# Buffers of the first MLP's first norms, the place of the down projection's last right operand, and late transposes behind the next mixer's projections

## The chip, the cores and the metric

One core of one Trainium2 chip. The metric is the time of one execution on the device in microseconds (us), as the median of three runs. TensorE (PE, with its weight loads as PEld), VectorE (DVE), ScalarE (ACT), GpSimd (POOL) and the DMA queue of SyncE (SP, or SPq) each work through a fixed list of instructions in order and wait for each other by semaphores.

## The reference

Two layers on 1024 tokens of width 1024, all in fp32. Each layer normalizes the stream, mixes tokens, adds the normalized result back, and does the same with an MLP of inner width 4096:

```python
for layer in range(DEPTH):
    u = rmsnorm(h, norm_mix_pre[layer])
    if layer % 2 == 0:
        mix = hybrid_ab_mixer(u, ...)      # gated delta rule beside an RWKV7 recurrence
    else:
        mix = retention_mixer(u, ...)      # chunkwise retention with rotary positions
    h = h + rmsnorm(mix, norm_mix_post[layer])
    u = rmsnorm(h, norm_mlp_pre[layer])
    f = jnp.square(jax.nn.relu(u @ mlp_w_up[layer])) @ mlp_w_down[layer]
    h = h + rmsnorm(f, norm_mlp_post[layer])
```

## The kernel before

**Products.** An fp32 factor is split into a rounded part (hi, a cast on ACT) and the rest (lo, a subtraction on DVE), `split_in` at L1174 and L1175; a product is three matmuls, hi by hi, lo by hi, hi by lo. The MLP multiplies in quarters with seven products in place of eight. Up projection: `product`, L1302 to L1304; its results go to DRAM as `hds[n]`. Down projection: seven products n in the order 1, 5, 6, 3, 7, 2, 4 (L1472). Each has eight steps h of 24 matmuls (`three`, L1444 to L1446): the left operand comes from `hds[n][h]` (L1517), the right one from `right(n, h)` (L1422), which loads blocks of `w_down` of 512 KB (`block`, L1419) and keeps running differences in R0 to R7 and B22, made by POOL (`plus`, L1413). Results are summed in `facc` (`flush`, also L1413).

**Norms.** The 1024 tokens are eight tiles of 128, here called tokens 0 to 7. After each mixer and each MLP a token goes through `post_norm_in`: load of the stream (L1181), square with sum on ACT (L240), small one-column operations on DVE (L244 to L248), multiply by the norm's weights on POOL (L1183), scale and add on DVE (L1184), store (L1185). Then `pre_norm`: square of the new stream on ACT, L266 on DVE, eight transposes on PE (L272), and the transposed tile is split into hi and lo for the next products. In MLP 0 `normed` first loads the mixer's output (`fd`, L1267), which the mixer stored at L1149.

**Generators.** `normed` and `finish` are generators; lists of tokens (`steps`, `end`, `behind`) say when each goes on between products.

**Memory.** `region((a, b))` names kilobytes a to b of each SBUF partition; an area deals them out, and a tile in used memory waits until the last users of the old one are done. Bounds of 8 KB units give the number in a tile's name (piece104 begins at 104 KB). The order of each engine's list, SP's loads and stores included, is fixed when the kernel is built, by a scheduler that plans by a cost model of its own.

## Time and profile before

| | |
|---|---|
| runs | 3387.65, 3390.89, 3395.80 us, median 3390.89 |
| profiled execution | 3386.39 us, of it span 3384.7 us |
| PE busy | 92% of the span |
| PEld, DVE, ACT, POOL busy | 79%, 59%, 39%, 39% |
| DMA | 423.72 MB, mean 125 GB/s |
| loads of `w_down` | 96 of 512 KB |

Times inside the kernel count from the start of the span. The layers follow each other: mixer 0 to about 1121 us, its norms to 1208, MLP 0 to 1850, mixer 1, and MLP 1 to the end, its up projection until 3040. In a view of windows a row gives busy time and, in brackets, the number of instructions for each engine, then the granted clock of PE as a share of 2.4 GHz (0.50 is 1.2 GHz), the DMA engines' share and rate. In a timeline a row gives start, length, engine, line, operation and, in square brackets, the idle time before it and what ended it.

### The profile page before, as it was taken

Reading aid. Unit: us, or ns where it says so; the run is one execution under the profiler, and the core shown is the slowest. Engines: PE = TensorE matmul, PEld = TensorE weight load, DVE = VectorE, ACT = ScalarE, POOL = GpSimd, SP = SyncE. Lnnn points to the kernel's source line nnn. Section 1 sums busy time; section 2 is a strip of 40 time slices with the busy share of each in tenths; the row PEclk is TensorE's granted clock in tenths of the full one; section 3 lists DMA queues with packets and bytes.
Section 4 is the critical chain, followed back from the end, with each engine's and each line's share of the span. In section 5 each row is a group of like instructions: output and inputs, shape, how many; then the busy total and the mean of one; then the engine's idle time right before and its main releaser. Section 6 shows DMA issues by size and latency. Waiting matters only on the chain.

```text
span 3384.7 us, 44433 instructions
## 1 busy us (share of the span) xinstructions
PE 3119.0 (92%) x16424; PEld 2661.3 (79%) x16424; DVE 1990.7 (59%) x3399; ACT 1311.8 (39%) x2336; POOL 1307.9 (39%) x1577
## 2 busy tenths in 40 slices
PE   8899899899998379999997999999999989999997
PEld 6677788787877258887886889998999968878885
DVE  6445555545633466557468665567655775547467
ACT  5332333323232345543334333334333355543333
POOL 1663363365520247657043111002110147657044
PEclk9898979988897689999998999999999989999998
DMA  5221222221241456566254322235222356566353
GB/s 165 66 66 35 71 61 63 67 55 52 61 119 54 146 155 191 184 239 251 100 193 164 116 81 82 88 107 162 82 81 88 106 177 195 179 242 236 104 187 137
DMA packets 401691, 423.72 MB, mean 125 GB/s; under 512 B 69569, under 2 KB 303937, under 8 KB 400961
## 3 DMA queue, kind: packets, MB, share of 16 engines
q1 hardware_dynamic: 401472, 420.88, 39.1%
q8 instruction: 129, 2.11, 0.3%
q14 instruction: 90, 0.73, 0.1%
HBM read 322.77 MB, written 98.04 MB: 124 GB/s over the span
## 4 chain that ended last, share of the span: by engine, by line
PE 52%; DVE 5%; DMA 4%; issue 1%; ACT 1%; POOL 1%; SPq 0%; DVEq 0%; ACTq 0%; POOLq 0%
PE bank L185 20%; PE bank L1445 5%; PE bank L1303 5%; PE bank L1444 5%; PE bank L1302 5%; PE bank L1446 5%; PE bank L1304 5%; DMA piece<-in_mlp_w_down_dram 1%; DVE piece L1175 1%; DMA piece<-ud 1%; DMA piece<-in_mlp_w_up_dram 1%; DMA piece<-hd 1%; DVE piece L1501 1%; POOL piece L1413 0%; DVE piece L205 0%
## 5 line engine op out<-in xcount | busy, mean ns | idle before, releaser
L185 PE MATMUL bank<-piece,piece 128*128 128x512 f32 (+7 forms) x10032 | 1751.0, 336 | 64.9 <-ACT piece L312 15.5
L185 PEld LDWEIGHTS bank<-piece,piece 128*128 128x128 f32 (+1 forms) x10032 | 1508.9, 200 | 275.4 <-issue 34.4
L1175 DVE TENSOR_TENSOR piece<-piece,piece 128x512 fp32r<-128x512 f32 (+2 forms) x436 | 581.1, 1357 | 268.3 <-ACT piece L1174 262.1
L1174 ACT CAST piece<-piece 128x512 fp32r<-128x512 f32 (+2 forms) x436 | 354.7, 838 | 565.5 <-PE bank L1303 212.8
L1302 PE MATMUL bank<-piece,piece 128*128 128x512 f32 x896 | 353.0, 395 | 15.2 <-ACT piece L1174 9.4
L1445 PE MATMUL bank<-piece,piece 128*128 128x512 f32 x896 | 354.1, 395 | 13.3 <-DVE piece L1175 13.3
L1303 PE MATMUL bank<-piece,piece 128*128 128x512 f32 x896 | 352.5, 393 | 1.9 <-DVE piece L1234 1.9
L1304 PE MATMUL bank<-piece,piece 128*128 128x512 f32 x896 | 349.9, 394 | 1.3 <-DVE piece L1175 1.2
L1446 PE MATMUL bank<-piece,piece 128*128 128x512 f32 x896 | 351.1, 393 | 0.0
L205 DVE TENSOR_TENSOR piece<-piece,piece 128x1024 fp32r<-128x1024 f32 x202 | 258.2, 1279 | 144.3 <-ACT piece L204 139.6
L1444 PE MATMUL bank<-piece 128*128 128x512 f32 x832 | 327.6, 394 | 15.3 <-ACT piece L1174 15.3
L204 ACT CAST piece<-piece 128x1024 fp32r<-128x1024 f32 x204 | 213.5, 1048 | 295.3 <-PE bank L185 275.8
L1413 POOL TENSOR_TENSOR piece<-piece,piece 128x1024 f32<-128x1024 f32 (+1 forms) x72 | 210.8, 2946 | 262.1 <-DMA piece<-in_mlp_w_down_dram 225.5
L620 POOL TENSOR_TENSOR piece<-piece 128x120 f32<-128x120 f32 (+22 forms) x496 | 183.6, 370 | 229.6 <-DMA piece<-dm 194.1
L1577 POOL TENSOR_TENSOR piece<-piece,piece 128x512 f32<-128x512 f32 x32 | 64.4, 2013 | 530.3 <-DVE piece L1576 475.8
L1302 PEld LDWEIGHTS bank<-piece,piece 128*128 128x128 f32 x896 | 170.4, 190 | 53.1 <-ACT piece L1174 10.4
L1445 PEld LDWEIGHTS bank<-piece,piece 128*128 128x128 f32 x896 | 171.2, 191 | 50.4 <-DVE piece L1175 14.4
L1183 POOL TENSOR_TENSOR piece<-piece,piece 128x1024 f32<-128x1024 f32 x28 | 78.5, 2812 | 330.4 <-ACT piece L240 199.3
L624 POOL TENSOR_TENSOR piece<-piece,piece 128x120 f32<-128x120 f32 (+22 forms) x496 | 190.1, 383 | 37.4
L1304 PEld LDWEIGHTS bank<-piece,piece 128*128 128x128 f32 x896 | 170.3, 190 | 38.2 <-DVE piece L1175 2.7
L1303 PEld LDWEIGHTS bank<-piece,piece 128*128 128x128 f32 x896 | 170.5, 190 | 37.6 <-DVE piece L1234 2.2
L1446 PEld LDWEIGHTS bank<-piece,piece 128*128 128x128 f32 x896 | 170.6, 190 | 35.1
(242 smaller groups left out, 3197.1 us busy)
## 6 DMA issues: line engine op xcount, KB each, us to landing
hd<-piece SPq DMA_DIRECT2D x208, 256.0 KB
piece<-hd SPq DMA_DIRECT2D x104, 512.0 KB
piece<-in_mlp_w_down_dram SPq DMA_DIRECT2D x96, 512.0 KB
piece<-in_ret_w_in_dram SPq DMA_DIRECT2D x96, 512.0 KB
piece<-in_mlp_w_up_dram SPq DMA_DIRECT2D x32, 1024.0 KB
piece<-in_ab_w_in_dram SPq DMA_DIRECT2D x60, 512.0 KB
piece<-in_ret_w_out_dram SPq DMA_DIRECT2D x32, 512.0 KB
h<-piece SPq DMA_DIRECT2D x24, 512.0 KB
```

The lines of the kernel that those rows point to most:

```text
L185: PE.matmul(ps, lhsT, rhs, start=start, stop=stop)
L204: ACT.copy(hi, raw)
L205: eng.tensor_tensor(out=lo, in0=raw, in1=hi, op=ALU.subtract)
L1174: ACT.copy(hi, src)
L1175: eng.tensor_tensor(out=lo, in0=src, in1=hi, op=ALU.subtract)
L1302: PE.matmul(ps, w[0][:, k, :], u[0][:, k, :], start=start and k == 0, stop=False, skip_group_check=True)
L1303: PE.matmul(ps, w[0][:, k, :], u[1][:, k, :], start=False, stop=False, skip_group_check=True)
L1304: PE.matmul(ps, w[1][:, k, :], u[0][:, k, :], start=False, stop=stop and k == 3, skip_group_check=True)
L1413: eng.tensor_tensor(out=out, in0=a, in1=b, op=op)
L1444: PE.matmul(ps, a[0], b[0], start=first, stop=False)
L1445: PE.matmul(ps, a[1], b[0], start=False, stop=False)
L1446: PE.matmul(ps, a[0], b[1], start=False, stop=last)
```

## The change

Three parts.

First norms of MLP 0: tokens 0 to 3 get buffers of their own (104 to 112 for `nf`, 112 to 120 for `nx`), tokens 4 to 7 keep those at 172 and 180. Layer 1 stays as it was.

Last right operand: the difference R[h] minus block (1, 0, h), which product 4 uses, is made in product 2, which loads the same block as its own right operand. Product 4 loads none; the loads of `w_down` fall from 96 to 80. In layer 1 the split of this operand moves into product 2 too; its left operand there has four buffers, not six. R0 to R3 now lie at 120 to 136 and R4 to R7 at 104 to 120, and the sums of tokens 4 to 7 at 72 to 88, those of tokens 0 to 3 at 88 to 104.

Late transposes: in MLP 0's last product tokens 4 and 5 no longer go as far as their transposes; the generators of tokens 4 to 7 are handed on in a list, and layer 1 takes one entry of it behind each of its first projections. Its tiles lie at other places, and its output tiles are made when first written. In PE's list the 24 matmuls of the first projection of layer 1 (q) now come ahead of the transposes of token 4, which stood ahead of them; the transposes of token 5 follow, then k.

```diff
--- before.py
+++ after.py
@@ -1198,15 +1198,16 @@
             bs = [region((a, a + 16)).area() for a in (140, 156)]
             b11, b21 = ([mk(a, [P, 4, HT], f"b{i}", F32R) for i in "HL"] for a in bs)
             if layer:
-                wrow, nrm, tmp = region((24, 32)).area(2), region((32, 40)).area(2), region((172, 180)).area()
-                nfa = None
+                wrow, tmp = region((24, 32)).area(2), region((172, 180)).area()
+                nrms = [region((32, 40)).area(2)] * 2
                 at = dict(t1=104, t2=120, t3=40, b22=56, t4=88)
                 ring = region((180, 204)).area(6)
                 raw_at, res_at, ops_at = (0, 16), (72, 88), ((40, 56), (180, 204), (56, 64))
                 left_at, norm_at = (0, 16), ((172, 180), (64, 72))
             else:
-                wrow, nrm, tmp = region((32, 40)).area(2), region((180, 188)).area(2), region((24, 32)).area()
-                nfa = region((172, 180)).area(2)
+                wrow, tmp = region((32, 40)).area(2), region((24, 32)).area()
+                nfas = [region((a, a + 8)).area(2) for a in (104, 172)]
+                nrms = [region((a, a + 8)).area(2) for a in (112, 180)]
                 at = dict(t1=104, t2=120, t3=188, b22=72, t4=88)
                 ring = region((40, 72)).area(8)
                 raw_at, res_at, ops_at = (172, 188), (0, 16), ((188, 204), (40, 72))
@@ -1263,10 +1264,10 @@
                 if layer:
                     f = late[t - 4]
                 else:
-                    f = mk(nfa, [P, D], "nf")
+                    f = mk(nfas[t // 4], [P, D], "nf")
                     SP.dma_start(f, fd[t])
                 junk = mk(tp, [P, HT], "junk").bitcast(BF16)
-                xt = post_norm_in(nrm, f, res, mid, t, w1, junk)
+                xt = post_norm_in(nrms[t // 4], f, res, mid, t, w1, junk)
                 yield
                 yield from pre_norm(f, xt, w2, (psx if t < 4 else psn, "pd"),
                                     to_pair(ug, t) if t < 4 else combine(t))
@@ -1396,14 +1397,15 @@
 
 
             sh = [P, 2, HT]
-            left = region(left_at, (16, 24)).area(6)
+            left = region(left_at, (16, 24)).area(6) if layer == 0 else region(left_at).area(4)
             stream = region((24, 40)).area(4)
             ring = region(*ops_at).area(6)
-            R = [mk(region((104, 136)).area() if 0 else at_, sh, f"R{i}") for at_ in [region((104, 136)).area()] for i in range(8)]
+            atr = region((120, 136), (104, 120)).area()
+            R = [mk(atr, sh, f"R{i}") for i in range(8)]
             at22 = region((140, 172)).area()
             B22 = [mk(at22, sh, f"B{i}") for i in range(8)]
             fp = region((72, 104)).area()
-            fp = region((72, 104)).area()
+            fp = region((88, 104), (72, 88)).area()
             facc = [mk(fp, [P, D], f"fa{t}") for t in range(8)]
             c11, c12 = ([facc[t][:, i * HT : i * HT + HT] for t in range(4)] for i in range(2))
             c21, c22 = ([facc[t + 4][:, i * HT : i * HT + HT] for t in range(4)] for i in range(2))
@@ -1434,10 +1436,15 @@
                     b = block(0, 1, h)
                     plus(POOL, b, B22[h], b, ALU.subtract)
                     return b
+                if n == 4:
+                    return R[h]
                 b = block(1, 0, h)
-                if n == 4:
-                    plus(POOL, R[h], R[h], b, ALU.subtract)
-                    return R[h]
+                plus(POOL, R[h], R[h], b, ALU.subtract)
+                if layer:
+                    hi, lo = mk(his, sh, f"bh{h}", F32R), mk(los, sh, f"bl{h}", F32R)
+                    ACT.copy(hi, R[h])
+                    DVE.tensor_tensor(out=lo, in0=R[h], in1=hi, op=ALU.subtract)
+                    parts.append((hi, lo))
                 return b
 
             def three(ps, a, b, first, last):
@@ -1469,7 +1476,10 @@
                 for i in range(t, max(t - 3, -1), -1):
                     next(run[i], None)
 
+            parts = []
             for n in (1, 5, 6, 3, 7, 2, 4):
+                if n == 2 and layer:
+                    his, los = region((140, 172)).area(), region((16, 24), (120, 136), (104, 112)).area()
                 if n == 2:
 
                     ugn = pair(region((140, 172)).area(), "u") if layer == 0 else None
@@ -1492,14 +1502,6 @@
                 pss = [mk(psd, [P, HT], "pd") for _ in range(4)]
                 if n == 4 and layer:
                     atl, athl = region(left_at).area(2), region(*ops_at).area(2)
-                    parts = []
-                    his, los = region((140, 172)).area(), region((16, 24), (104, 128)).area()
-                    for h in range(8):
-                        b = right(4, h)
-                        hi, lo = mk(his, sh, f"bh{h}", F32R), mk(los, sh, f"bl{h}", F32R)
-                        ACT.copy(hi, b)
-                        DVE.tensor_tensor(out=lo, in0=b, in1=hi, op=ALU.subtract)
-                        parts.append((hi, lo))
                     for t in range(4):
                         raw = mk(atl, [P, 16, P], "a")
                         SP.dma_start(raw, hq[:, t])
@@ -1526,23 +1528,24 @@
                             if n == 2:
                                 end(t)
                             elif n == 4:
-                                end(t + 4)
+                                for i in range(t + 4, max(t + 2, 3), -1):
+                                    next(run[i])
                 if n == 2:
                     for t in (3, 2, 3):
                         next(run[t], None)
-            return ugn, [run[i] for i in (7, 6, 7)]
+            return ugn, [[run[7], run[4]], [run[5]], [run[6]], [run[7]]]
 
 
     def layer1(ug, behind, late, meanwhile):
         if True:
-            rest, early = region((72, 136)), region((40, 72))
+            rest, early = region((96, 136)), region((40, 72))
+            fp, Sp = region((72, 88)).area(1), region((88, 96)).area(1)
             yp, Yp, sp = region((0, 24)).area(3), region((24, 32)).area(2), region((136, 140)).area(1)
             wp[0] = region((32, 40)).area(2)
             weight_area(172, 204)
             cp, tp = early.area(1), early.area(2)
-            fp, hp = rest.area(1), rest.area(2)
-            f = [mk(fp, [P, D], f"rf{t}") for t in range(4)]
-            late.extend(f)
+            hp = rest.area(2)
+            f = []
             psj, psc, pst = bank_area(4, 5, 6), bank_area(1, 2, 3), bank_area(7, 0)
             us = tiles(ug)
             tabs = {}
@@ -1557,7 +1560,7 @@
 
             def table(c, i, n):
                 return tabs[c][:, i : i + n]
-            S = [mk(fp, [P, 256], f"S{h}") for h in range(NH_RET)]
+            S = [mk(Sp, [P, 256], f"S{h}") for h in range(NH_RET)]
             lg = np.log1p(-np.exp2(-5.0 - np.arange(NH_RET, dtype=np.float32))).astype(np.float32)
 
             def project(c0):
@@ -1603,6 +1606,9 @@
                         mm(ps, gH[:, kk % 2, tt], wh[:, kk, :], kk == 0, False)
                         mm(ps, gL[:, kk % 2, tt], wh[:, kk, :], False, False)
                         mm(ps, gH[:, kk % 2, tt], wl[:, kk, :], False, kk == 3)
+                    if not f:
+                        f.extend(mk(fp, [P, D], f"rf{i}") for i in range(4))
+                        late.extend(f)
                     if h == 1:
                         ACT.copy(f[t][:, cc], ps)
                     else:
@@ -1631,7 +1637,7 @@
 
             def step():
 
-                for gen in steps.pop(0) if steps else ():
+                for gen in behind.pop(0) if behind else steps.pop(0) if steps else ():
                     next(gen, None)
 
             for hf in range(2):
@@ -1642,14 +1648,8 @@
 
                     q = rope(P * h, hf, "q")
                     step()
-                    while behind:
-                        next(behind.pop(0), None)
-                        if len(behind) == 1:
-                            break
                     k = rope(1024 + P * h, hf, "k")
                     step()
-                    while behind:
-                        next(behind.pop(), None)
                     qd, t = split(hp, [P, NCH, P], "qd"), mk(tp, [P, NCH, P], "ropet")
                     POOL.tensor_tensor(
                         out=t, in0=q.rearrange("p (j t) -> p j t", t=P),
```

What this does to the lists, at three places.

SP, the norms between mixer 0 and MLP 0 (fd0 to fd7 are the mixer's output of tokens 0 to 7, h1 the new stream), before:

```order
L1185 DMA h1_0_9_77<-piece180_45_7733 128x1024
L1149 DMA fd4_37_105<-piece96_19_452 128x512
L1185 DMA h1_1_10_78<-piece180_45_7733 128x1024
L1149 DMA fd5_38_106<-piece88_18_450 128x512
L1181 DMA piece180_45_7733<-in_x_dram 128x1024
L1149 DMA fd6_39_107<-piece88_18_450 128x512
L1149 DMA fd7_40_108<-piece88_18_450 128x512
L1267 DMA piece172_43_7730<-fd2_35_103 128x1024
L1185 DMA h1_2_11_79<-piece180_45_7733 128x1024
L1181 DMA piece180_45_7733<-in_x_dram 128x1024
L1267 DMA piece172_43_7730<-fd3_36_104 128x1024
```

and with the change:

```order
L1185 DMA h1_0_9_77<-piece112_45_7733 128x1024
L1149 DMA fd4_37_105<-piece96_19_452 128x512
L1185 DMA h1_1_10_78<-piece112_45_7733 128x1024
L1149 DMA fd5_38_106<-piece88_18_450 128x512
L1268 DMA piece172_46_7914<-fd4_37_105 128x1024
L1181 DMA piece112_45_7733<-in_x_dram 128x1024
L1149 DMA fd6_39_107<-piece88_18_450 128x512
L1268 DMA piece172_46_7914<-fd5_38_106 128x1024
L1149 DMA fd7_40_108<-piece88_18_450 128x512
L1268 DMA piece104_43_7730<-fd2_35_103 128x1024
```

The loads of tokens 4 and 5 (L1268) stand ahead of the one of token 2, in buffers at 172; before, they came after the stores of tokens 2 and 3.

SP, in the mixer's second half (yd is the recurrence's output, in_x_dram the stream that the norms add to), with the change:

```order
L1149 DMA fd0_33_101<-piece88_18_450 128x512
L198 DMA piece32_7_215<-in_ab_w_out_dram 128x2x512
L1181 DMA piece112_45_7733<-in_x_dram 128x1024
L1149 DMA fd1_34_102<-piece88_18_450 128x512
L1131 DMA piece88_18_450<-yd10_51_119 128x512
L1268 DMA piece104_43_7730<-fd0_33_101 128x1024
L1181 DMA piece112_45_7733<-in_x_dram 128x1024
L1149 DMA fd2_35_103<-piece96_19_452 128x512
L1131 DMA piece88_18_450<-yd11_52_120 128x512
L1268 DMA piece104_43_7730<-fd1_34_102 128x1024
```

and PE's list there, from the last read of the old tile at 112 (the second operand of the first row) to the transposes of L531:

```order
L185 MATMUL bank5_6_74<-piece64_15_432,piece112_21_568 128x128
L185 MATMUL bank5_6_74<-piece172_29_713,piece64_15_432 128x64
L185 MATMUL bank5_6_74<-piece196_32_1300,piece64_15_432 128x64
...
L185 MATMUL bank1_2_70<-piece48_12_258,piece8_1_197 128x512
L185 MATMUL bank5_6_74<-piece96_19_452,piece56_14_413 128x512
L185 MATMUL bank7_8_76<-piece196_32_1300,piece136_24_613 128x64 x2
L531 MATMUL bank4_5_73<-ident_124_192,piece196_32_1300 128x128 x4
```

The two loads of the stream into 112 and the two of `fd` into 104 are new at this place; before, they went to 180 and 172, the former ahead of the last load of yd, the latter behind it.

SP, the turn of MLP 0 from up to down projection (six loads of `w_down`, to 148, 24 and 140, stand ahead of these rows), before:

```order
L1419 DMA piece128_76_10304<-in_mlp_w_down_dram 128x2x512
L1419 DMA piece120_75_10303<-in_mlp_w_down_dram 128x2x512
L1317 DMA hd73_110_178<-piece0_67_8488 128x512
L1517 DMA piece16_87_10315<-hd14_63_131 128x1024
L1517 DMA piece16_87_10315<-hd15_64_132 128x1024
L1317 DMA hd53_94_162<-piece0_67_8488 128x512
L1419 DMA piece120_75_10303<-in_mlp_w_down_dram 128x2x512
L1419 DMA piece128_76_10304<-in_mlp_w_down_dram 128x2x512
L1317 DMA hd63_102_170<-piece0_67_8488 128x512
L1317 DMA hd33_78_146<-piece8_68_8489 128x512
L1419 DMA piece112_74_10302<-in_mlp_w_down_dram 128x2x512
L1419 DMA piece104_73_10301<-in_mlp_w_down_dram 128x2x512 x2
```

and with the change:

```order
L1421 DMA piece128_76_10304<-in_mlp_w_down_dram 128x2x512
L1421 DMA piece120_75_10303<-in_mlp_w_down_dram 128x2x512
L1318 DMA hd73_110_178<-piece0_69_8490 128x512
L1421 DMA piece120_75_10303<-in_mlp_w_down_dram 128x2x512
L1421 DMA piece128_76_10304<-in_mlp_w_down_dram 128x2x512
L1318 DMA hd53_94_162<-piece0_69_8490 128x512
L1519 DMA piece16_89_10317<-hd14_63_131 128x1024
L1519 DMA piece16_89_10317<-hd15_64_132 128x1024
```

R0 and R1 lay in piece104, the eleventh to thirteenth loads of `w_down` being one of 112 and these two; they now lie in piece120, the eighth and ninth.

## Rows read from the trace of the kernel before

**Rows 1.** Page, part 1: busy us, share of the span, instructions of each engine.

```profile
PE 3119.0 (92%) x16424; PEld 2661.3 (79%) x16424; DVE 1990.7 (59%) x3399; ACT 1311.8 (39%) x2336; POOL 1307.9 (39%) x1577
```

**Rows 2.** Windows: length, busy time (instructions) of PE, PEld, DVE, ACT, POOL; PEclk, DMA share, GB/s.

```profile
1700.00:1750.00 50.00, 50.00 (x223) 41.39 (x222) 36.55 (x27) 19.08 (x20) 23.90 (x11) 1.00 0.58 192
1500.00:1550.00 50.00, 42.30 (x180) 34.59 (x179) 23.36 (x19) 20.83 (x26) 24.82 (x13) 0.93 1.03 393
3000.00:3100.00 100.00, 92.35 (x395) 75.83 (x394) 53.98 (x44) 44.45 (x59) 59.38 (x30) 0.95 0.82 300
1800.00:1820.00 20.00, 13.70 (x50) 10.74 (x49) 17.68 (x30) 10.69 (x18) 10.23 (x4) 0.80 0.27 95
3310.00:3360.00 50.00, 35.51 (x139) 28.00 (x139) 43.35 (x52) 16.97 (x24) 28.98 (x8) 0.86 0.39 137
3230.00:3240.00 10.00, 10.00 (x45) 8.28 (x45) 9.29 (x4) 4.01 (x4) 10.00 (x5) 1.00 0.63 212
```

**Rows 3.** Timeline, one round of MLP 0's first norms (start us, us, what, [idle before])

```profile
1134.41 1.97 PE L272 MATMUL bank<-ident,piece 128*128 128x128 f32 x8 [12.61 <-DVE piece L266]
1136.40 0.32 SPq L1267 DMA_DIRECT2D piece<-fd  x1
1140.74 1.06 ACT L240 ACTIVATE piece<-piece 128x1024 bf16<-128x1024 f32 x1 [3.74 <-DMA piece<-fd]
1141.97 2.34 POOL L1183 TENSOR_TENSOR piece<-piece,piece 128x1024 f32<-128x1024 f32 x1 [10.60 <-ACT piece L240]
1147.35 1.97 PE L272 MATMUL bank<-ident,piece 128*128 128x128 f32 x8 [10.97 <-DVE piece L266]
```

**Rows 4.** Timeline of PE, token 4's transposes and MLP 0's first matmul.

```profile
1172.92 1.94 PE L272 MATMUL bank<-ident,piece 128*128 128x128 f32 x8 [10.71 <-DVE piece L266]
1208.45 0.79 PE L1302 MATMUL bank<-piece,piece 128*128 128x512 f32 x1 [3.39 <-ACT piece L1174]
```

**Rows 5.** Timeline of PE, end of layer 0's mixer.

```profile
1089.51 8.44 PE L185 MATMUL bank<-piece,piece 128*128 128x512 f32 x24 [3.93 <-ACT piece L312]
```

**Rows 6.** Timeline of SP and PE, and one step of the chain, at MLP 0's turn.

```profile
1504.83 3.42 SPq L1419 DMA_DIRECT2D piece<-in_mlp_w_down_dram  x4
1519.23 8.46 DMA piece<-in_mlp_w_down_dram
1528.82 0.79 PE L1444 MATMUL bank<-piece 128*128 128x512 f32 x1 [7.70 <-ACT piece L1174]
```

**Rows 7.** Chain that ended last, at MLP 1's turn: start us, us, what.

```profile
3038.81 8.47 DMA piece<-in_mlp_w_down_dram
```

**Rows 8.** Timeline of POOL and PE, last product of MLP 0.

```profile
1795.52 2.40 POOL L1413 TENSOR_TENSOR piece<-piece,piece 128x1024 f32<-128x1024 f32 x1 [3.48 <-DMA piece<-in_mlp_w_down_dram]
1805.87 0.80 PE L1445 MATMUL bank<-piece,piece 128*128 128x512 f32 x1 [2.96 <-DVE piece L1175]
```

**Rows 9.** Timeline of PE at layer 1's start; line L246 there (ns min/median/max).

```profile
1866.95 1.97 PE L272 MATMUL bank<-ident,piece 128*128 128x128 f32 x8 [17.10 <-DVE piece L266]
L246 DVE TENSOR_TENSOR mt<-mr x6: 150/160/2316, 1853.3 to 1867.5; 128x1 f32<-128x1 f32 x6
```

**Rows 10.** Timelines, last product of MLP 1; line L1413 from 3230 (ns min/median/max).

```profile
3306.45 13.60 DVE L1501 TENSOR_TENSOR piece<-piece,piece 128x1024 fp32r<-128x1024 f32 x6
3320.56 1.22 DVE L1501 TENSOR_TENSOR piece<-piece,piece 128x1024 fp32r<-128x1024 f32 x1
3351.73 0.80 PE L1445 MATMUL bank<-piece,piece 128*128 128x512 f32 x1 [3.02 <-DVE piece L1175]
L1413 POOL TENSOR_TENSOR piece<-piece,piece x13: 2273/3087/3389, 3227.9 to 3313.4; 128x1024 f32<-128x1024 f32 x11, 128x512 f32<-128x512 f32 x2
```

**Rows 11.** Waits of SP, 1030 to 1215 (us, times, longest); timelines of SP, PE.

```profile
SPq L1267 <- DVE rs_t L228: 58.8, 1, 58.8
1082.71 0.80 SPq L1267 DMA_DIRECT2D piece<-fd  x2
1003.07 0.60 PE L531 MATMUL bank<-ident,piece 128*128 128x128 f32 x4
```

## The prediction

> **What bounds the kernel now.** The page's busy shares come first: the reader is to see that TensorE (PE) works 92% of the span [rows 1], so time can only come out of the stretches in which it starves. Next come the windows [rows 2]. Where nothing starves it, PE starts 222 matmuls of 128x512 in 50 us (223 are listed in 1700:1750, one of them reaching in from before), that is 0.2252 us each. A stretch with fewer has lost the difference times 0.2252, idle time and low granted clock together. Six such stretches touch the change: the norms ahead of MLP 0 (1130 to 1210, where PE has little but transposes), the turn from up to down projection in both MLPs (1500:1550, 3000:3100), the last down product in both (1800:1820, 3310:3360), and the start of layer 1 (1850 to 1867). For each I then read the chain of waits or the timeline: what ended last before PE went on. Little else is to be won: 3119 of 3385 us are work.
>
> The profiled execution took 3386.39 us (span 3384.7, 1.7 us outside it), 4.5 below the median of the runs, 3390.89. The sum is made against the former and carried over to the latter. About 0.2% (6.8 us) is what a measurement of this kernel can tell from no change.
>
> **The change, part by part.**
>
> *1. First norms of MLP 0.* A round goes from one token's transposes to the next's in 12.94 us: transposes at 1134.41, only then the load of the mixer's output into the freed buffer at 1136.40, ScalarE's square at 1140.74, POOL's multiply at 1141.97, the next transposes at 1147.35 [rows 3]. The in-order ScalarE has the post-norm square of token n+1 ahead of the pre-norm square of token n, so each token waits for the next one's load, and this for token n-1's transposes. With tokens 4 and 5 in buffers of their own, their loads stand ahead of token 2's on SP and their squares wait for no transposes. Tokens 1 and 2 stay (token 3's load still waits for token 1), but the two rounds that bring tokens 3 and 4 no longer hold a load. What remains of a round is POOL's start to transposes, 5.38 us [rows 3], or 6.61 counted from ScalarE's square. I take the shorter, since the squares now run ahead: 2 x (12.94 - 5.38) = 15.1. With the longer it is 12.7; if only one round falls, 6.3; if tokens 2 and 3 came closer too, 22. The 35.5 us from token 4's transposes to the first matmul of the up projection [rows 4] stay. The added SBUF reuse (the operand t1 of MLP 0 lies at 104) waits for token 3, which is done before token 4 and so hides it.
> Beside it: ScalarE has a square and a table load of token 0 between two casts that PE needs, and PE waits 3.93 us [rows 5]. They move ahead of both casts. I take 2 (0 to 2.5). Against it: three loads of 512 KB leave together; at 393 GB/s [rows 2] one takes 1.33 us, and I charge 1.5 (0 to 3). SP now meets token 0's two loads early, between the stores of the mixer's output; I charge 1 (0 to 8, see the third rival). **Sum 15 (6 to 22).**
>
> *2 and 3. Up to down.* PE stops until the first right operand R0 is cast: 7.70 us idle, then low clock [rows 6]. The window has 180 matmuls, 42 short: 9.5 us; in MLP 1 395 of 444, 11.0 us [rows 2]. R0 was the twelfth load from w_down, issued at 1519.23 and 8.46 us on its way; the loads before it leave from 1504.83 on [rows 6]. At 104 it is now loaded eighth, in the slot that ended the four loads at 1504.83 to 1508.25. Issued at some 1507.9 with the same 8.46 it lands at 1516.4, its cast is done by 1518, and PE is through with the up projection at 1521.1, which is 7.70 before 1528.82. So the wait goes and with it most of the slow start. The left operand is no next bound: it was loaded before R0. In MLP 1 the same 8.47 us stands at the end of the chain [rows 7]. **8.5 each (4 to 9.5 and 4 to 11)**; the low end is if loads share the queue's rate so that R0 gains only half its wait.
>
> *4. Last product of MLP 0.* POOL's last subtraction waits 3.48 us for its load and runs to 1797.9; the norms' multiplies queue behind it, and PE waits 2.96 us for a split queued behind their VectorE work [rows 8]. The window shows 50 of 89 starts; 39 x 0.2252 = 8.8 us [rows 2]. The subtractions now fall in product 2, which has those blocks loaded anyway, and the eight loads of the last product are gone (sixteen with MLP 1). Product 2 gains eight subtractions of POOL, which has time there; nothing else is added. Some 2 us remain for the transposes that stand in this stretch in both. **6.5 (3 to 8).**
>
> *5. Late transposes.* PE stands 17.10 us, until 1866.95, for the scaling of token 4 [rows 9]. In the new order q's 24 matmuls, 24 x 0.2252 = 5.4 us, run in that gap, since their operands (tokens 0 to 3, weights) exist. But q's rope adds VectorE and POOL work ahead of the scaling; a one-column VectorE operation takes up to 2.32 us beside POOL's multiply instead of 0.16 [rows 9]. I subtract 1.5. k then waits for token 5. **4 (0 to 9).**
>
> *6. Last product of MLP 1.* 139 of 222 starts in 3310:3360, 83 x 0.2252 = 18.7 us lost [rows 2]. POOL's subtractions go one by one behind their loads, VectorE's splits follow (six in 13.60 us beside POOL, 1.22 alone, [rows 10]), and the left operand's split queues behind those. All of it moves into product 2; no load is left on the path. What stays: the third left operand waits for a buffer and then for a cast and a split, 3.02 us now [rows 10], with its slow clock about 3.7. The price is product 2, where PE takes 24 x 0.2252 = 5.41 us per step of h, VectorE now has three splits, and POOL one subtraction, 2.34 alone by its multiply of the same size [rows 3], 3.09 in the median of this stretch [rows 10]. In 3230:3240 POOL was busy all 10 us and VectorE did four operations in 9.29, with PE full [rows 2]: 4 x 1.22 + (10 / 3.09) x 2.34 = 12.5 us of lone work in 10. A step of product 2 is 3 x 1.22 + 2.34 = 6.0, at that rate 4.8 us. It fits, with a tenth to spare, but the sums of product 7 come on top: I charge 2. Left buffers fall from six to four, still two steps ahead. **18.7 - 3.7 - 2 = 13 (2 to 16).**
>
> The Trainium skill, "SBUF — State Buffer", section "SBUF: two separate sides", speaks against this part: VectorE operations with two SBUF inputs and POOL operations share a port pair that is locked for a whole instruction, so they would run one after the other. The one-column operation of 2.32 us agrees with it; the window with 12.5 us of lone work in 10 does not bear it out in full. By the rule a step takes 6.0 us against 5.41, 8 x 0.6 = 4.8 us lost in place of 2, and part 6 gives 10.
>
> The tail behind the last matmul is the same. Sum: 15 + 8.5 + 8.5 + 6.5 + 4 + 13 = 55.5 us; 3386.4 - 55.5 = 3330.9 for a profiled execution, 3390.9 - 55.5 = **3335 us** for the median.
>
> **The rivals.**
> *First, product 2 of MLP 1 becomes bound by VectorE and POOL (chance 0.16).* If each of the three splits takes the 2.27 us that six of them took on average [rows 10], a step is 6.8 us: 8 x (6.8 - 5.41) = 11 us lost. For it: two engines near their end in 3230:3240. Against it: PE was full there. Part 6 falls to 4, total 3344.
> *Second, the turns only shift (0.14).* In 1500:1550 the DMA share is 1.03 at 393 GB/s: the queue, not the order, would be the bound, and after R0 the later operands come late. Against it: the steps need 1 MB per 5.41 us, half that rate. Parts 2 and 3 give 4 each, total 3344. The Trainium skill, "DMA: Bandwidth & Descriptors", section "Where 436 GB/s comes from", gives a ceiling near 435 GB/s for all queues together; the 393 is close to it, which agrees.
> *Third, slower: SP's queue blocks (0.04).* SP is in order. The loads of tokens 0 and 1 went out at 1082.71, after 58.8 us in which SP waited for the recurrence [rows 11] with all that was needed issued. Now they stand ahead of loads and stores of the mixer's second half, and wait for the last PE read of SBUF at 112. If that came with the end of the recurrence too, at 1082.7, all behind would be held from 1003 on, 80 us; it decides from a hold of 56 us on, and a full one gives 3391 + 80 - 55 = 3416. Against it: in PE's order that read is 23 instructions ahead of the transposes by L531 that the trace has at 1003.07 [rows 11]. So SP is held till 1003 at most, 8 us.
> *Fourth, the rounds stay (0.09).* If ScalarE's or VectorE's new order keeps a late square ahead of token 3, part 1 gives 2: total 3348.
> *Fifth, two or more of these at once, or losses that nothing here shows (0.05): 3355 to 3395.*
>
> **How the numbers follow.** The forecast has 0.52; its own range, half of the way to the bounds summed up (36 us less gain, 20 more), is 3325 to 3353. The first, second and fourth rivals lie at 3344 to 3348 and, with smaller losses elsewhere, reach 3360. With every gain at its high end it would be 3315; not all come at once, and 3316 is as far as I go. The range 3316 to 3361 leaves out the third and fifth rivals and a tail on either side. Faster by over 0.2%: 0.52 + 0.16 + 0.14 + 0.09, and most of the fifth, 0.94. Within it: 0.02. Slower: 0.04.
>
> **What would show it.** Token 4's transposes 14 to 16 us after token 2's instead of 25.6; no wait of L1444 for L1174 above 2 us at either turn; 85 or more starts in the twenty microseconds after product 4 of MLP 0 begins; q's matmuls before token 4's transposes in layer 1; in the last 75 us a full PE but for some 3 us. Starved steps in product 2 of MLP 1 would prove the first rival, a late R1 or B22 at the turns the second, an SP wait of tens of microseconds near 1000 the third. The prediction is wrong if the total gain is under 30 us.

## The result, and the profile after

The change is faster, and the forecast was close: 3335.3 us in the median of 4 runs (3332.77 to 3347.88) against 3389.27 for the kernel before (4 runs), ratio 0.9852 (95% interval 0.9814 to 0.9889; a ratio here is taken over the runs themselves and is not the quotient of the two medians). A second comparison, of 6 runs with 11, gave 3346.72 against 3390.84 us, ratio 0.9864 (0.9833 to 0.9896): 54 and 44 us. The profiled execution took 3332.98 us (span 3331.3), 53.4 below the 3386.39 of the profile before.

Line numbers have moved by one to seven: `plus` and `flush` are L1415, `block` L1421, `three` L1451 to L1453, the norms' load of `fd` L1268, the up projection L1303 to L1305, the rotary operations L1577 to L1580. On the page of the change, part 1:

```profile
PE 3099.7 (93%) x16424; PEld 2647.8 (79%) x16424; DVE 2001.2 (60%) x3399; ACT 1309.2 (39%) x2336; POOL 1318.4 (40%) x1577
```

The same 16424 matmuls keep PE busy 19.3 us less than in [rows 1], since fewer run at the low clock (the mean granted clock is 0.945, before 0.936); the rest of the gain is idle time. The windows of the change are put so that each stands to the end of its up projection (the first two) or its down projection (the next two) as the one of [rows 2] did; the last is from product 7 of MLP 1, as the last one there is (product 2 is shown under step 6 below). Columns as there:

```profile
1476.40:1526.40 50.00, 47.27 (x201) 38.32 (x200) 28.78 (x21) 22.32 (x28) 26.58 (x13) 0.97 1.04 394
2960.20:3060.20 100.00, 95.48 (x409) 78.19 (x408) 61.88 (x45) 46.20 (x61) 62.28 (x30) 0.97 0.80 292
1763.30:1783.30 20.00, 18.13 (x85) 14.85 (x84) 19.53 (x40) 13.03 (x24) 8.67 (x4) 1.00 0.25 90
3256.60:3306.60 50.00, 47.31 (x209) 38.87 (x208) 32.71 (x44) 17.89 (x24) 19.84 (x6) 1.00 0.48 166
3190.00:3200.00 10.00, 10.00 (x46) 8.29 (x45) 9.51 (x5) 3.08 (x4) 10.00 (x4) 1.00 0.58 178
```

Against [rows 2] the turn of MLP 0 starts 21 matmuls more (201 against 180), that of MLP 1 only 14 more (409 against 395), the last product of MLP 0 35 more (85 against 50) and that of MLP 1 70 more (209 against 139). Times 0.2252 us this is 4.7, 3.2, 7.9 and 15.8 us. In the last row VectorE and POOL are nearly full and PE is too.

The norms, timeline of PE from token 1's transposes to the first up matmul, then of ScalarE ahead of the first, with the change and, in the last line, before (token 0's transposes began at 1105.55, before at 1120.76):

```profile
1123.16 1.97 PE L272 MATMUL bank<-ident,piece 128*128 128x128 f32 x8 [16.58 <-DVE piece L266]
1139.04 1.97 PE L272 MATMUL bank<-ident,piece 128*128 128x128 f32 x8 [13.92 <-DVE piece L266]
1144.71 1.97 PE L272 MATMUL bank<-ident,piece 128*128 128x128 f32 x8 [3.70 <-DVE piece L266]
1149.10 1.94 PE L272 MATMUL bank<-ident,piece 128*128 128x128 f32 x8 [2.42 <-DVE piece L266]
...
1183.80 0.79 PE L1303 MATMUL bank<-piece,piece 128*128 128x512 f32 x1 [3.66 <-ACT piece L1174]
...
1116.55 1.06 ACT L240 ACTIVATE piece<-piece 128x1024 bf16<-128x1024 f32 x1 [9.24 <-DMA piece<-fd]
...
1127.80 1.06 ACT L240 ACTIVATE piece<-piece 128x1024 bf16<-128x1024 f32 x1 [5.27 <-DMA piece<-fd]
```

From token 2 (1139.04) to token 4 (1149.10) it is 10.1 us where it was 25.6. But the two rounds ahead of that, which nothing was to change, grew from 13.7 and 12.9 us (transposes at 1120.76, 1134.41 and 1147.35 before, two of them in [rows 3]) to 17.6 and 15.9: ScalarE now waits 9.24 us for a load where it waited 5.27, and in the second round POOL's two multiplies come back to back (4.64 us from 1130.71, where one took 2.34). Three loads of `fd`, 512 KB each, had left at 1106.62, 1108.44 and 1109.65. If the square waited for the last of them, it came 6.9 us behind that load's issue, where the round in [rows 3] has 4.3; how much of the 9.24 is the place in SP's list and how much the crowd of loads was not tried.

Of mixer 0 one thing more, the end of its recurrence, windows of the change:

```profile
1040.00:1050.00 10.00, 9.51 (x72) 8.68 (x71) 3.85 (x11) 1.61 (x8) 0.00 (x0) 1.00 0.01 2
1050.00:1060.00 10.00, 9.87 (x76) 8.97 (x75) 4.36 (x13) 3.29 (x19) 0.00 (x0) 1.00 0.00 1
```

and of the same kernel in another profile (`after_again`, below):

```profile
1040.00:1050.00 10.00, 9.89 (x73) 8.75 (x71) 3.81 (x9) 1.35 (x7) 0.00 (x0) 1.00 0.00 0
1050.00:1060.00 10.00, 10.00 (x39) 8.61 (x39) 2.21 (x7) 1.46 (x7) 0.00 (x0) 0.52 0.01 2
```

The same program does 76 matmuls in one and 39 in the other: the granted clock fell to 1.2 GHz. PE had been full until then (9.89 of 10 us), in the last microseconds with narrow matmuls, most of 32 to 128 columns. From 1000 to 1105 us the mean granted clock is 0.92 or 0.93 in five of the twelve profiles of the table below (before_again, the change, only_early, late_places, rope_third), whose mixer 0 averages 1113.3 us, and 0.76 to 0.79 (before: 0.77) in the other seven, 1129.1 us. Each of the two kernels has shown both. So the time to token 0's transposes differs between profiles of one kernel, and is kept apart below.

### The profile page after: what moved, and what is told of

Same layout as the page of the kernel before. It is cut to its first block, busy times and chain, and to the rows that moved or that the text cites. A ratio compares the mean times of both kernels' runs of the same rounds, so it can differ in the third digit from the quotient of the medians.

```text
span 3331.3 us, 44407 instructions
## 1 busy us (share of the span) xinstructions
PE 3099.7 (93%) x16424; PEld 2647.8 (79%) x16424; DVE 2001.2 (60%) x3399; ACT 1309.2 (39%) x2336; POOL 1318.4 (40%) x1577
## 5 line engine op out<-in xcount | busy, mean ns | idle before, releaser
L185 PE MATMUL bank<-piece,piece 128*128 128x512 f32 (+7 forms) x10032 | 1738.9, 335 | 69.4 <-ACT piece L312 15.9
L1175 DVE TENSOR_TENSOR piece<-piece,piece 128x512 fp32r<-128x512 f32 (+2 forms) x436 | 599.4, 1401 | 223.9 <-ACT piece L1174 219.7
L1303 PE MATMUL bank<-piece,piece 128*128 128x512 f32 x896 | 352.9, 394 | 12.6 <-ACT piece L1174 11.1
L1453 PE MATMUL bank<-piece,piece 128*128 128x512 f32 x896 | 350.6, 392 | 2.3 <-DVE piece L1175 2.3
L1305 PE MATMUL bank<-piece,piece 128*128 128x512 f32 x896 | 348.4, 393 | 0.3 <-DVE piece L1175 0.3
L1451 PE MATMUL bank<-piece 128*128 128x512 f32 x832 | 321.6, 392 | 1.9 <-ACT piece L1174 1.9
L1415 POOL TENSOR_TENSOR piece<-piece,piece 128x1024 f32<-128x1024 f32 (+1 forms) x72 | 215.5, 3012 | 256.2 <-DMA piece<-in_mlp_w_down_dram 205.0
L1580 POOL TENSOR_TENSOR piece<-piece,piece 128x512 f32<-128x512 f32 x32 | 64.5, 2014 | 535.3 <-DVE piece L1579 451.6
L1303 PEld LDWEIGHTS bank<-piece,piece 128*128 128x128 f32 x896 | 170.1, 190 | 49.2 <-ACT piece L1174 12.2
L1452 PEld LDWEIGHTS bank<-piece,piece 128*128 128x128 f32 x896 | 169.6, 189 | 46.7 <-DVE piece L1175 11.5
L1453 PEld LDWEIGHTS bank<-piece,piece 128*128 128x128 f32 x896 | 169.7, 189 | 38.2 <-DVE piece L1175 2.8
L1305 PEld LDWEIGHTS bank<-piece,piece 128*128 128x128 f32 x896 | 170.1, 190 | 37.2 <-DVE piece L1175 1.5
```

The costliest lines, as they stand in the source:

```text
L185: PE.matmul(ps, lhsT, rhs, start=start, stop=stop)
L1175: eng.tensor_tensor(out=lo, in0=src, in1=hi, op=ALU.subtract)
L1303: PE.matmul(ps, w[0][:, k, :], u[0][:, k, :], start=start and k == 0, stop=False, skip_group_check=True)
L1305: PE.matmul(ps, w[1][:, k, :], u[0][:, k, :], start=False, stop=stop and k == 3, skip_group_check=True)
L1415: eng.tensor_tensor(out=out, in0=a, in1=b, op=op)
L1451: PE.matmul(ps, a[0], b[0], start=first, stop=False)
```

## The experiments

Each run left a profile, cut here into stages: to the start of token 0's transposes (mixer 0), to the first up matmul (norms), the up projection of MLP 0, its down projection with the norms' part in it, layer 1's mixer up to the last up matmul of MLP 1, and the down projection of MLP 1, to its last matmul. The tail of some 10 us behind that is the same in all. In us:

| kernel | mixer 0 | norms | up 0 | down 0 | layer 1 + up 1 | down 1 |
|---|---|---|---|---|---|---|
| before | 1120.8 | 87.6 | 312.3 | 328.8 | 1190.9 | 334.2 |
| before_again | 1115.0 | 87.2 | 314.2 | 328.3 | 1193.3 | 333.8 |
| the change | 1105.5 | 78.3 | 313.3 | 315.7 | 1187.8 | 320.6 |
| after_again | 1124.7 | 77.6 | 313.9 | 316.8 | 1187.9 | 319.1 |
| only_norms | 1129.9 | 78.1 | 314.1 | 329.4 | 1191.6 | 333.5 |
| only_order | 1138.2 | 87.3 | 314.7 | 323.3 | 1191.2 | 333.6 |
| only_early | 1123.4 | 86.8 | 314.1 | 321.1 | 1190.9 | 322.3 |
| only_late | 1134.2 | 87.1 | 312.6 | 329.8 | 1186.1 | 334.3 |
| without_late | 1132.7 | 77.6 | 314.1 | 317.4 | 1192.3 | 320.6 |
| rope_second | 1123.2 | 78.3 | 315.7 | 315.0 | 1186.9 | 321.4 |
| late_places | 1116.8 | 77.7 | 313.8 | 317.1 | 1193.6 | 319.7 |
| rope_third | 1106.0 | 78.3 | 316.1 | 314.9 | 1194.3 | 319.0 |

Mixer 0 varies by 33 us and hides in a median of runs what a part of 5 to 9 us does. Each other stage agrees within 4 us, mostly within 2, wherever its code is the same, so the parts are read from them.

**Each part alone**, the others put back as before.

*only_norms*: the buffers of the first norms alone.

```diff
...
-                nfa = region((172, 180)).area(2)
+                nfas = [region((a, a + 8)).area(2) for a in (104, 172)]
+                nrms = [region((a, a + 8)).area(2) for a in (112, 180)]
...
```

> The kernel before with the two pairs of buffers for MLP 0's first norms alone. Theory: the norms alone are worth some 9 us (mixer's last matmul to the first up matmul 78 us instead of 87.5), and the 12 to 15 us by which the mixer itself ended earlier in the changed kernel came with a granted clock of 1.00 instead of 0.50 during the recurrence's last 30 us. Rival: the new order of the mixer's lists keeps the clock up, so that this kernel shows both every time, first up matmul at 1184 instead of 1208, total 25 us faster (ratio 0.9927). If the clock is a matter of the single execution, the first up matmul comes at 1184 or at 1199, total 9 to 25 us faster. Nothing behind MLP 0's first matmul changes.

Measured 3388.07 us against 3385.97 for the kernel before (10 and 31 runs, as for the next three), ratio 0.998 (0.9954 to 1.0006). The norms took 78.1 us, 9 less, and the down projection nothing less; mixer 0 took 1129.9 us at the low clock, so the rival, a mixer that is faster every time, fell. The 9 us are this part's; the 15 that the forecast had are not there, here or in any other profile.

*only_order*: R0 to R3 at 120, R4 to R7 at 104.

```diff
-            R = [mk(region((104, 136)).area() if 0 else at_, ...
+            atr = region((120, 136), (104, 120)).area()
+            R = [mk(atr, sh, f"R{i}") for i in range(8)]
...
```

> The kernel before with R0 to R3 at 120 and R4 to R7 at 104 alone. Theory: only the two turns from up to down projection change. By the trace of the changed kernel they give 4 us in MLP 0 and 3 us in MLP 1, since part of the wait moves to later steps of the first product: 7 us, ratio 0.998. Rival, the forecast: 8.5 each, 17 us, ratio 0.995; the waits at later steps would then belong to the smaller number of left buffers, which is unchanged here.

Measured 3382.04 us, 0.9985 (0.9948 to 1.0022). MLP 0 gained 5.8 us (323.3 against a mean of 329.1 in the four profiles without this part and without the next), MLP 1 0.4; the run's own theory had 4 and 3, its rival 8.5 each. PE's waits in the second down product (product 5) of its MLP 1, and last the wait at the first down matmul before, timelines:

```profile
3106.68 0.50 PE L1446 MATMUL bank<-piece,piece 128*128 128x512 f32 x1 [1.74 <-DVE piece L1175]
3113.85 1.20 PE L1445 MATMUL bank<-piece 128*128 128x512 f32 x4 [2.34 <-ACT piece L1174]
3119.93 0.80 PE L1446 MATMUL bank<-piece,piece 128*128 128x512 f32 x1 [4.88 <-DVE piece L1175]
...
3048.40 0.79 PE L1444 MATMUL bank<-piece 128*128 128x512 f32 x1 [7.65 <-ACT piece L1174]
```

Before, that wait of 7.65 us was all the idle time of the turn. It is gone, and 8.96 us in three waits some 50 us on have taken its place: product 5 takes 54.7 us instead of 43.5. In MLP 1 the turn only shifts, as in the second rival.

*only_early*: the last right operand made in product 2 (in layer 1 with its split and with four left buffers).

```diff
+                if n == 4:
+                    return R[h]
                 b = block(1, 0, h)
-                if n == 4:
-                    plus(POOL, R[h], R[h], b, ALU.subtract)
-                    return R[h]
+                plus(POOL, R[h], R[h], b, ALU.subtract)
...
```

> The kernel before with the last right operand made in product 2 alone (R0 to R7 in their old places). Theory: 8 us in the last product of MLP 0 and 11 us in that of MLP 1, less nothing elsewhere: 19 us, ratio 0.9944; in MLP 1's product 2 waits of PE of 2 us in all. Rival, VectorE and POOL bind product 2 of MLP 1: waits there of 5 us or more and a total gain under 14 us.

Measured 3373.39 us, 0.9957 (0.9928 to 0.9986): 8.0 us less in MLP 0 and 11.7 in MLP 1, both near the forecast's 6.5 and 13. In MLP 1 the last product fell from 61.8 us (mean of the five profiles without this part) to 48.3, but product 2 grew from 43.5 to 46.7, with one wait of 2.05 us. Of the 11.7, some 1.7 are a shorter wait at the first down matmul (6.70 us against a mean of 8.4 in the four profiles of the old order without this part), which nothing in this part explains.

*only_late*: the late lists and layer 1's places.

```diff
...
-            return ugn, [run[i] for i in (7, 6, 7)]
+            return ugn, [[run[7], run[4]], [run[5]], [run[6]], [run[7]]]
...
```

> The kernel before with the late transposes behind the next mixer's projections alone (with its buffers in layer 1). Theory: q's matmuls run in the gap, but the scaling of token 4 comes some 5 us later, so layer 1's start gives nothing: same or 1 to 3 us slower there; MLP 0's last product gains 0 to 2. Total within 4 us, ratio 0.999 to 1.001. Rival, the forecast: 4 us faster. It also tells whether the 6 us that the up projection of MLP 1 gained in the changed kernel (324 to 318 us) belong to this part: then they show here, total 6 us faster.

Measured 3385.74 us, 0.9999 (0.9969 to 1.0029). Its stage is 1186.1 us against 1190.9 to 1193.6 in the seven profiles of the table without the late lists. It gains 4.8 to 7.5 us there, but PE's wait for token 4 is 17.02 us: not where the forecast looked. Three further runs went into that.

**Both kernels again, and the change without its third part.** `before_again` and `after_again` have no edit; `without_late` is the change with the edit of only_late undone.

> The kernel before once more, for a second profile. Theory: token 0's transposes anywhere between 1105 and 1140 us (1120.8 in the first profile), all stages behind them as in the first: 87 us of norms, down projections of 329 and 334 us, layer 1 867 us. Rival: 1121 again within 2 us, the mixer's time being the kernel's own.

> The changed kernel once more, unaltered. In the profiles so far the time of mixer 0, up to token 0's transposes, lies between 1105 us (changed kernel) and 1138 us (kernels whose mixer 0 is the same in code), and everything behind it agrees within 1 or 2 us where the code does. Theory: this spread is the single execution's (granted clock of the recurrence), so that here token 0's transposes come anywhere between 1105 and 1140, the stages behind are as in the first profile of the changed kernel (78 us of norms, down projections of 316 and 321 us), and the ratio over many runs settles at 39 us of steady gain and what mixer 0 makes of it, 0.984 to 0.990. Rival: the changed kernel's mixer 0 is faster by itself: again near 1105.

> The changed kernel with the third part undone: transposes of tokens 4 to 7 ahead of and behind the first projection as before, with layer 1's old buffers. Theory: layer 1 has 867 us again instead of 870 and the up projection of MLP 1 323 instead of 318; all other stages stay. 2 to 3 us slower than the changed kernel in the steady stages. Rival, if the late part gave nothing at all: both together 1188 us as in the changed kernel.

Measured: 3383.57 us for `before_again` (one run), 3346.72 (0.9864) for `after_again`, 3359.63 (3355.44 to 3366.88), 0.9899 (0.9857 to 0.9941), for `without_late`. The two intervals overlap and the medians cannot tell the parts apart; the stages give 1192.3 against 1187.9. Token 0's transposes came at 1115.0 and 1124.7 us, so neither rival (1121 again, 1105 again) held, and every stage behind them repeats within 3 us. At the start of layer 1 the change itself shows, on PE and then on VectorE (timelines):

```profile
1812.98 5.60 PE L185 MATMUL bank<-piece,piece 128*128 128x512 f32 x24
1835.53 4.00 PE L272 MATMUL bank<-ident,piece 128*128 128x128 f32 x16 [16.95 <-DVE piece L266]
...
1827.63 2.10 DVE L246 TENSOR_TENSOR mt<-mr 128x1 f32<-128x1 f32 x2
1829.70 1.25 DVE L247 SCALAR_TENSOR_TENSOR mt<-mt,ms 128x1 f32<-128x1 f32 x2
1830.92 2.33 DVE L248 SCALAR_TENSOR_TENSOR mr<-mt,mr 128x1 f32<-128x1 f32 x2
1833.22 2.25 DVE L266 SCALAR_TENSOR_TENSOR piece<-piece,mr,piece 128x1024 f32<-128x1024 f32 x1
```

q fills its 5.6 us, and the wait behind it is as long as before, 16.95 against 17.10 [rows 9]. Token 4 is ready 22.4 us after MLP 0's last matmul, not 17.1: q's three rotary operations on VectorE and POOL's part of them come ahead, and six one-column operations beside POOL take 5.7 us (0.16 each alone).

**rope_second and rope_third: the rotary operations behind the late step.** q and k of the first head are both projected first, then the late step, then their rotary operations.

```diff
...
-                    q = rope(P * h, hf, "q")
+                    pre = [None, None]
+                    if behind:
+                        pre = [project(P * h), project(1024 + P * h)]
+                        step()
+                    q = rope(P * h, hf, "q", pre[0])
...
```

In `rope_second` the late transposes write over the banks in which q and k wait, so these two of the first head are not the reference's; the amount of work is the same. `rope_third` projects them into other banks (`mk(psc, ...)`).

> The changed kernel, where for the first head of layer 1 the projections q and k are both issued first, then the late norms' next step, and only then the rotary operations of q and k on VectorE and POOL. Theory: in the changed kernel the scaling of token 4 came 22.4 us behind the last product instead of 17.1, since q's rotary operations and the POOL operations that lock VectorE out stood ahead of it, so the 5.4 us of q were paid back. Here the scaling comes 17 to 18 us behind the product again, and q and k fill 10.8 us of that gap: layer 1 takes 860 to 864 us instead of 870, the whole 6 to 10 us less. Rival: the rotary operations are missed later by as much, and layer 1 stays at 868 to 870.

> The change, with q and k of the first head both projected ahead of the first late step, into the other three banks of PSUM, and their rotary operations behind it. Theory 1 (what a shorter wait gives, the slow clock behind it takes back): PE's wait for token 4's scaling falls from 17 to some 7 us, as it did in the kernel that projected into the usual banks, but the clock stays at its low level for longer, and layer 1 takes 868 to 870 us, no less than in the change. Theory 2 (that kernel lost its gain by its banks): layer 1 takes 860 to 864 us, and the run is 5 to 8 us faster than the change.

Measured 3349.89 us, 0.9878 (0.9846 to 0.991), and 3347.63 us, 0.987 (0.9824 to 0.9916): neither is faster than the change. Timeline of PE in `rope_second` and, last, in `after_again`:

```profile
1832.41 11.04 PE L185 MATMUL bank<-piece,piece 128*128 128x512 f32 x48
1850.12 1.97 PE L272 MATMUL bank<-ident,piece 128*128 128x128 f32 x8 [6.66 <-DVE piece L266]
...
1858.31 2.08 PE L185 MATMUL bank<-piece 128*128 128x128 f32 x8 [6.22 <-POOL piece L1580]
...
1855.43 1.97 PE L272 MATMUL bank<-ident,piece 128*128 128x128 f32 x8 [16.55 <-DVE piece L266]
```

The window of 50 us from MLP 0's last matmul, of `rope_second`:

```profile
1832.20:1882.20 50.00, 35.54 (x203) 31.73 (x202) 36.99 (x66) 22.70 (x41) 14.96 (x8) 0.80 0.50 160
```

and the same window of `after_again`:

```profile
1833.00:1883.00 50.00, 32.29 (x201) 28.89 (x201) 38.28 (x66) 22.45 (x41) 16.49 (x8) 0.83 0.47 152
```

The wait for token 4 fell from 16.55 us (`after_again`) to 6.66, but one of 6.22 for the rotary sum came behind it. PE was busy 3.25 us longer for two matmuls more, since the clock stood lower (0.80 against 0.83). What the shorter idle time gave, the slow clock took. `rope_third` had waits of 11.25 and 1.82 us there (theory 1 had said 7 for the first), and layer 1's mixer took 871.8 us, against 868.3 to 869.8 in the profiles of the change and 868.9 in `rope_second`: no gain in either, as `rope_second`'s rival and `rope_third`'s theory 1 had it.

**late_places: the places of the third part without its lists.**

```diff
...
-            return ugn, [[run[7], run[4]], [run[5]], [run[6]], [run[7]]]
+            return ugn, [run[i] for i in (7, 6, 7)]
...
```

> The change with the new places of layer 1's tiles kept and the lists put back: tokens 4 and 5 go to their transposes in the last product of MLP 0 again, so those of token 4 stand ahead of q in PE's list, as before. The third part gave 4 to 5 us when layer 1 and the up projection of MLP 1 are taken together (1187 to 1188 us with it, 1191 to 1193 without it in the profiles so far). Theory 1, the lists make it (where the late steps stand sets the list of the up projection of MLP 1 too): layer 1 plus up projection 1191 to 1193, the run some 5 us slower than the change, 3350 to 3362. Theory 2, the places make it (the output tiles lie alone, made when first written): 1187 to 1188, and no difference from the change in the run.

Measured 3345.2 us (3326.91 to 3350.95), 0.9836 (0.9787 to 0.9885): in the median not slower than the change, against theory 1. Its stage, 1193.6 us, is what theory 1 said, and mixer 0's spread hides 5 us in a median of four. PE's waits in its up projection of MLP 1, timeline:

```profile
2697.76 0.80 PE L1305 MATMUL bank<-piece,piece 128*128 128x512 f32 x1 [0.82 <-DVE piece L1175]
2732.57 0.79 PE L1303 MATMUL bank<-piece,piece 128*128 128x512 f32 x1 [2.26 <-ACT piece L1323]
2745.10 0.50 PE L1303 MATMUL bank<-piece,piece 128*128 128x512 f32 x1 [1.96 <-ACT piece L1234]
2747.32 0.80 PE L1304 MATMUL bank<-piece,piece 128*128 128x512 f32 x1 [1.72 <-DVE piece L1235]
```

and in `after_again`:

```profile
2725.21 0.66 PE L272 MATMUL bank<-ident,piece 128*128 128x128 f32 x4 [0.52 <-DVE piece L1235]
2743.60 1.11 PE L272 MATMUL bank<-ident,piece 128*128 128x128 f32 x4 [5.93 <-DVE piece L1235]
```

The waits add up to much the same, 6.8 and 6.5 us, but they are spread in one and gathered in the other, where the last transposes also stand 12 matmuls earlier in PE's list. The 75 us from the first up matmul, of `late_places` and then of `after_again`:

```profile
2695.70:2770.70 75.00, 68.21 (x280) 54.28 (x281) 54.83 (x73) 42.23 (x79) 36.72 (x25) 0.89 0.55 170
2701.30:2776.30 75.00, 68.29 (x297) 55.41 (x298) 53.52 (x73) 43.10 (x81) 38.75 (x27) 0.92 0.55 170
```

PE is busy for the same time, but at a granted clock of 0.89 against 0.92, and starts 280 matmuls against 297: 17 x 0.2252 = 3.8 us. Those 12 matmuls sort all kernels of which the lists were compared: the change, only_late and rope_second have them, and take 1186.1 to 1187.9 us; before, only_order, without_late, late_places and rope_third, whose late lists are the change's, have not, and take 1190.9 to 1194.3. So the gain goes with where the scheduler puts these transposes a whole mixer later, not with q in the gap (`rope_third` has q and k there and not the gain). That their place is the cause is argued from this sorting; which of the scheduler's rules makes the difference was not tried.

## Why the prediction was right, and which steps were not

The direction and the place of five of the six gains held, and the time was in the range. The sum was too large by about 15 us. Means over the profiles with and without a part give: norms 87.2 to 78.0, 9.2 us; MLP 0's down projection 329.1 to 316.2, 12.9; MLP 1's 334.0 to 320.1, 13.9; layer 1 with the up projection behind it 1192.0 to 1187.3 (the two rope kernels left out), 4.7; the up projection of MLP 0 nothing. That is **40.7 us** where the forecast had 55.5, and 3390.9 - 40.7 = 3350. It lies in both measured intervals (40.7 of 3390 is a ratio of 0.988) and in the forecast's range. That the first comparison gave 54 us, all but the forecast, was luck as far as the runs show, and has to do with mixer 0: the profile of the change had 1105.5 us there, 15.2 less than the one before, and the profile of the same kernel in the second comparison 1124.7. Of the difference between the two first spans, 53.4 us, these 15.2 are no proven effect of the change: with the new norms mixer 0 averages 1119.8 us over seven profiles, without them 1126.3 over five, in a spread of 33. (Among the profiles at the higher clock, and among those at the lower, the ones with the new norms are 10 and 3 us ahead; the waits account for 1.5 of this, see step 1, and the rest is open.)

*Step 1, 15 forecast, 9.2 measured.* The two rounds of tokens 3 and 4 fell by more than forecast, 25.6 to 10.1, 15.5 us in place of 15.1. (The sign given under "What would show it", 14 to 16 us, does not go with its own term: 25.6 - 15.1 leaves 10.5.) The charge of 1.5 (0 to 3) for three loads leaving together was the term that was mis-sized: the rounds of tokens 1 and 2 grew by 6.9 us in sum, behind a wait of 9.24 us for a load. The 2 us for ScalarE's table load and square ahead of the casts lie in mixer 0, outside the 9.2, but the waits themselves can be read there. With the change, timeline of PE and then of SP:

```profile
1071.90 1.11 PE L531 MATMUL bank<-ident,piece 128*128 128x128 f32 x4 [4.29 <-DVE piece L1053]
1074.51 8.23 PE L185 MATMUL bank<-piece,piece 128*128 128x512 f32 x24 [1.49 <-ACT piece L312]
...
995.45 0.34 SPq L1181 DMA_DIRECT2D piece<-in_x_dram  x1
1002.43 0.50 SPq L1268 DMA_DIRECT2D piece<-fd  x1
```

The wait of 3.93 us [rows 5] is 1.49 to 1.50 in all seven profiles with the new norms and 3.89 to 4.05 in the five without; the wait ahead of it rose from 3.3 or 3.4 to 4.29, so some 1.5 us are gained. The third rival, SP held for 56 us or more, did not happen: the four early loads left between 995.45 and 1002.43, with no more than 3.3 us between one entry of SP's list and the next. The 1 us charged for SP cannot be told from the clock's spread.

*Steps 2 and 3, 8.5 each forecast.* The wait of 7.70 us is gone in MLP 0, and the window has 21 of the 42 missing matmuls back, 4.7 us (5.8 by only_order): waits of 0.41 and 2.32 us follow, with some slow clock. In MLP 1 the window has 14 of the 49 back, 3.2 us, and only_order 0.4. The waits behind it in the change are these:

```profile
3030.00 1.20 PE L1451 MATMUL bank<-piece 128*128 128x512 f32 x4 [1.86 <-ACT piece L1174]
3033.86 0.79 PE L1452 MATMUL bank<-piece,piece 128*128 128x512 f32 x1 [2.66 <-DVE piece L1175]
```

and POOL there waits for a load (timeline):

```profile
3024.21 8.51 POOL L1415 TENSOR_TENSOR piece<-piece,piece 128x1024 f32<-128x1024 f32 x3 [5.46 <-DMA piece<-in_mlp_w_down_dram]
```

while the DMA engines are full (view of transfers, 3005 to 3035):

```profile
DMA packets 5714, 11.91 MB, mean 397 GB/s; under 512 B 421, under 2 KB 933, under 8 KB 5712
```

The step's "the left operand is no next bound" looked at one operand; the next bound is the stream of blocks behind R0. "Half that rate" in the second rival held for the steps by themselves, but the loads share the queue with the up projection's stores and product 1's left operands, at 397 GB/s without a gap. The rival's chance of 0.14 was too low for MLP 1. Why the order keeps some 3 us beside step 6 and next to nothing alone was not tried.

*Step 4, 6.5 forecast, 7.9 to 8.0 measured.* As said; one wait of 1.87 us for transposes is left, close to the 2 us that the step left there.

*Step 5, 4 forecast, 4.7 measured, by another way.* This step failed although its number came out. It said that q's matmuls run in a gap of 17 us and take 5.4 from it, less 1.5 for rotary operations ahead of the scaling. The gap moved by the whole of q: the charge should have been some 5.3 us, the delay of token 4's scaling. The 4.7 us came in the up projection of MLP 1. The Trainium skill, "SBUF — State Buffer", section "SBUF: two separate sides", says that a VectorE operation with two SBUF inputs and a POOL operation lock each other out for a whole instruction; the pairs of one-column operations of 2.10 and 2.33 us in the timeline above, beside POOL's multiplies, agree with it.

*Step 6, 13 forecast, 10.5 measured.* Before, 18.7 us were lost in its window [rows 2]; now 13 of 222 starts are missing, 2.9 us, close to the 3.7 left for the third left operand (one wait of 2.69 us). The term that was mis-sized is product 2. Windows of product 2 of MLP 1, before and with the change, and of the 10 us around its two waits (0.36 and 2.00 us, both for a split by L1175):

```profile
3269.00:3312.60 43.60, 43.60 (x194) 36.05 (x193) 28.22 (x16) 19.96 (x19) 23.71 (x10) 1.00 0.50 179
3226.80:3274.90 48.10, 45.74 (x193) 37.00 (x192) 36.87 (x28) 21.40 (x22) 21.63 (x9) 0.96 0.33 110
3236.00:3246.00 10.00, 7.83 (x34) 5.79 (x32) 9.97 (x4) 3.86 (x4) 9.05 (x4) 1.00 0.46 157
```

It took 48.1 us instead of 43.6: 2.4 of idle time, the rest slow clock behind it (0.96). In the seven profiles with this part it took 46.2 to 48.1 us, in the five without 43.5 to 43.7, so it pays 3.7 in the mean against the 2 charged. The last product fell by 14.2 in the mean (61.8 to 47.6), and 14.2 - 3.7 = 10.5. The prediction took its pace from 3230:3240, which lies in product 7 (3225.5 to 3269.0), where PE was full; the helpers fell behind only in product 2. The first rival, product 2 bound by both at 11 us lost, did not come in that size. The rule of the Trainium skill named in the prediction gave 4.8 us for product 2 and 10 for the part, which is close to what was measured: splits by L1175 (128x1024) in product 2 took up to 3.41 us while POOL worked, and 1.21 to 1.23 once its last subtraction there was over, and POOL's subtractions in product 2 took 3.3 to 3.5, against 2.34 for its multiply of the same size alone [rows 3]. No run isolates the lock as the cause.

The fourth rival, rounds that stay, fell with the 10.1 us from token 2 to token 4.

## What to carry to other kernels

Price a wait that is taken away by what arrives next on the same queue or engine: of four such waits here two went for good (the last products, one of them for 3.7 us in the product that took over its work), one went by half and one came back, most of it, in pieces some 30 to 65 us later. Work put into a gap ahead of the operation that ends it delays that operation too, if it sends work to the engine on which it runs; count the delay on that engine, not on the one with the gap. A pace read from ten microseconds of one product need not hold in the next, whose work is another. And when the sum agrees with the measured total, check it stage by stage: here 15 us too much in the sum were met by 15 us of another stage, in which the waits show 1.5 us of gain and the granted clock differs from one execution to the next.

## What the runs showed of the hardware that was not expected

- PE's granted clock fell to 1.2 GHz in the last part of mixer 0 with PE full before it and after it, in some profiles and not in others of the same kernel (39 and 76 matmuls in the same 10 us). Mixer 0 averages 1113.3 us in the five profiles at the higher clock and 1129.1 in the seven at the lower.
- Idle time and slow clock trade: `rope_second` waited 3.7 us less than `after_again` at the start of layer 1 in its two longest waits (6.66 and 6.22 against 16.55), and started 2 matmuls more in the 50 us, at a granted clock of 0.80 against 0.83.
